# Down projections of the second layer's experts as three float32r products, with the weights' low parts made on GpSimd

## The chip, the cores and the metric

The kernel runs on one core of a Trainium2 chip. The metric is the device time of one launch in microseconds (us). Five engines work side by side, each through its own instructions in order: TensorE (PE, with its weight loads as PEld), VectorE (DVE), ScalarE (ACT), GpSimd (POOL) and SyncE (SP, which here only issues loads). Semaphores order them against each other.

## The reference

Two layers work on 512 latent tokens of width 1024. Each layer has a token mixer (pooling, then attention) and a mixture of 16 SwiGLU experts, of which every token uses two. The change lies in the last line of the mixture, in the second layer only:

```python
def hier_moe(h, w_rg, b_rg, w_re, b_re, w_gate, w_up, w_down):
    ...
    a = jnp.einsum('nd,edf->nef', hf, w_gate)
    b = jnp.einsum('nd,edf->nef', hf, w_up)
    hid = jax.nn.silu(a) * b * gates.astype(h.dtype)[..., None]
    return jnp.einsum('nef,efd->nd', hid, w_down).reshape(shp)
```

An expert is 1024 to 2 x 256 (gate and up) and 256 to 1024 (down), in float32.

## The kernel before

The mixture of a layer (class `Moe`, method `experts`) takes the 16 experts one after the other. In the second layer each expert gets a block of `n` = 96 rows, fetched by index from a copy of the tokens in DRAM (`fetch`, an indirect DMA that GpSimd issues).

**Gate and up.** They are not multiplied in float32. Rows and weights are each split into a high part, rounded to float32r, and a low part, the float32 value less its high part (`split`: ScalarE casts, VectorE or GpSimd subtracts). Three float32r products (high by high, high by low, low by high; `mm3`, L475 to L477) stand for one float32 product. For one expert that is 8 x 3 = 24 products of 512 columns. The weights come as two 1 MB loads, and `ups_steps` splits them in four units of 128 x 1024 into a ring of six buffers, one expert ahead. The rows are turned (8 transposes, L466) and split by `turn`.

**Down.** `turn_hidden` turns the 96 x 256 hidden block into `hT` (two transposes, L767, and one copy by ScalarE, L769). `down` multiplies it with the expert's 1 MB of down weights in float32 (L783: two halves of 512 columns, two products each; the profile shows every float32 product as two MATMUL rows), VectorE multiplies the result with the layer's gate row (L784), and GpSimd issues an indirect DMA that adds the 96 rows to the output in DRAM (L785, called the scatter here; the fetch is L735). Every scatter of this layer adds to the same output, so each waits until the one before has landed.

**The order of a pass.** Pass `e` of the loop in `experts` writes, for each engine, in this order: the first two splits of expert `e + 1`; the 24 products of `up(e)`; the last two splits; the activation and the multiplication of hidden `e`; the fetch for expert `e + 3`; turning and splitting the rows of `e + 1`; `down(e - 1)`; and `turn_hidden(e)`. Every second pass VectorE also builds the one-hot tables that place the next two experts' rows (L713). Each engine keeps this order, so an instruction that waits holds back what is behind it on its engine. SyncE's weight loads are issued when `done` frees a slot of 1 MB.

Of the kernel before, what the change touches and what calls it, by code (L numbers as in the profile page):

```python
# [11 lines left out]
F32R = mybir.dt.float32r  # L12
# [8 lines left out]
D = 1024  # L21
# [7 lines left out]
NE = 16  # L29
# [196 lines left out]
def backbone(ctx: ExitStack, tc: tile.TileContext, a: dict, out: bass.AP):  # L226
    nc = tc.nc
    V, A, G, T = nc.vector, nc.scalar, nc.gpsimd, nc.tensor
# [76 lines left out]
    def done(*key):  # L305
        ar.used.remove((slots.pop(key), SLOT))
        fill()

    def get(*key):
        assert key in slots, key  # L310
        return live[key]
# [68 lines left out]
    for c in range(0, 512 + D, 512):  # L380
        hi = partA[0:64, :]
# [87 lines left out]
    def split(hi, lo, src, eng=V):  # L469

        A.copy(hi, src)  # L471
        eng.tensor_sub(lo, src, hi.bitcast(F32))  # L472
# [12 lines left out]
    class Moe:  # L485
# [277 lines left out]
        def turn_hidden(self, hid):  # L763
            n = self.n
            p = pb.get("t", [128, 2, n])
            for k in range(2):
                T.transpose(p[:, k, :], hid[:, k * 128:k * 128 + 128], ident[:n, :n])  # L767
            hT = self.sb.tile([128, 2, n], name="hidT", bufs=2)
            A.copy(hT, p)  # L769
            return hT  # L770

        def down(self, e, hT, wd):
            n = self.n
            y = self.sb.tile([128, D], name="y", bufs=2)[:n]
            gs = self.g2[0][:n]
            if self.l == 0:
                gs = y
                V.scalar_tensor_tensor(gs, self.g2[1], self.slots[e][2], self.g2[0], op0=OP.mult, op1=OP.add)
            for half in range(2):
                cols = slice(512 * half, 512 * half + 512)  # L780
                p = pb.get("y", [n, 512])
                for k in range(2):
                    T.matmul(p, hT[:, k, :], wd[:, k, cols], start=k == 0, stop=k == 1)  # L783
                V.tensor_mul(y[:, cols], p, gs[:, cols])  # L784
            G.indirect_dma_start(out=self.acc[e % len(self.acc)], out_offset=bass.IndirectOffsetOnAxis(ap=self.slots[e][0], axis=0),  # L785
                                 in_=y, in_offset=None, bounds_check=self.nt * 128 - 1, oob_is_err=False,
                                 compute_op=OP.add)

        def experts(self, acc, caps, more, hooks={}):
            l, nt, sb, mb = self.l, self.nt, self.sb, self.mb  # L790
# [22 lines left out]
            hT = {}  # L813
            for e in range(NE):
                cap(caps[min(e, len(caps) - 1)])
                first = ahead if e == 0 else iter(())
                ahead = group(2) if e == 0 else group(e + 3) if e % 2 and e + 3 < NE else iter(())
                if e:
                    next(ahead, None)
                behind = self.ups_steps(e + 1) if e + 1 < NE else iter(())  # L820
                next(behind, None)
                next(behind, None)

                def later():
                    yield from first
                    if e == 0:
                        yield next(ahead)
                    yield from behind

                hid = self.up(e, self.units.pop(e), later())  # L830
                next(ahead, None)
                for k in range(2 if e == 0 else e + 3, min(e + 4, NE)):
                    self.fetch(k)
                if e + 1 < NE:
                    self.turn(e + 1)
                if e < 2:
                    for _ in range(BESIDE[self.l] if e == 0 else 99):
                        next(more, None)
                if e:
                    self.down(e - 1, hT[e - 1], get("wd", l, e - 1))  # L840
                    done("wd", l, e - 1)
                hT[e] = self.turn_hidden(hid)
                if e == 2:
                    self.count()
                if e in hooks:
                    hooks[e]()
            self.down(e, hT[e], get("wd", l, e))
            done("wd", l, e)
            if NE in hooks:
                hooks[NE]()  # L850

# [6 lines left out]
            units = self.ring[-4:]  # L858
            nb = nc.values_load(self.nb[0:1, 0:1], min_val=0, max_val=2 * nt * 128 // self.n)  # L859
            with tc.For_i(0, nb) as _:  # L860
# [14 lines left out]
                wd = load(a["moe_wd"][l, bass.ds(ev, 1)].rearrange("o p n -> (o p) n"), 2)  # L875
# [16 lines left out]
                    pass  # L892
                self.fetch(NE)
                self.turn(NE)
                self.down(NE, self.turn_hidden(self.up(NE, units)), wd)
                V.tensor_scalar(blk, blk, 1.0, None, op0=OP.add)


# [30 lines left out]
    parts = 0  # L929
# [235 lines left out]
    hT = [hbuf[2], hbuf[3]] + hbuf  # L1165
# [128 lines left out]
    for i in range(17):  # L1294
        kv, t = divmod(i, 4)
        if i < 16:
            p = P[i] = pb.get("q", [128, 256])
# [63 lines left out]
    def wo_mm(p, half, t, k):  # L1361
# [6 lines left out]
    units = [(kv, pair, qh, hh, q2) for kv in range(4) for pair in range(2) for qh in range(2)  # L1368
             for hh in range(2) for q2 in range(2)]
    PT, Ps, mx, po = {}, {}, {}, {}  # L1370
    for step in range(len(units) + 8):
# [3 lines left out]
        if step < len(units):  # L1375
# [4 lines left out]
            p = pb.get("s", [128, 768])  # L1380
            for c0, c1 in ((0, 512), (512, 768)):
                for j in range(2):
                    T.matmul(p[:, c0:c1], qT[kv][:, 2 * pair + hh, q0:q0 + 128], kT[:, kv, j, c0:c1],  # L1383
                             start=j == 0, stop=j == 1)
# [10 lines left out]
        if 3 <= step <= len(units) + 2:  # L1395
# [4 lines left out]
            for g3 in range(2):  # L1400
                p2 = pb.get("t", [128, 3, 128])
                for j in range(3):
                    k = 3 * g3 + j
# [5 lines left out]
        if 7 <= step < len(units) + 7:  # L1409
# [4 lines left out]
            for k in (((), (0, 1), (2, 3), (4, 5)) if qh == 0 else ((0, 1), (2,), (3, 4), (5,)))[quarter]:  # L1414
                for hh in range(2):
                    T.matmul(po[g // 2][64 * hh:64 * hh + 64, 256 * qh:256 * qh + 256],  # L1416
                             vv[:, k, kv * 64:kv * 64 + 64], PT[g, hh][:, k, :],
                             start=k == 0, stop=k == NT - 1, skip_group_check=True)
# [28 lines left out]
    with ar.scope() as sb:  # L1447
# [25 lines left out]
        for t in range(4):  # L1473
            p = pb.get("q", [128, 512])
# [75 lines left out]
```

## Time and profile before

| | |
|---|---|
| median of 3 runs | 923.98 us (922.69 to 924.25) |
| profiled execution, its own time | 923.87 us |
| its span, first to last instruction | 922.1 us |
| busy in the span: PE, PEld, DVE, ACT, POOL | 87%, 59%, 67%, 52%, 18% |
| mean granted TensorE clock | 0.937 |
| second layer's expert loop | about 740 to 908 us of the span |

Busy shares are means over stages that have different limits. What decides a stage is which wait ends last in it, so the rows below are of the second layer's expert loop, and of two earlier places where GpSimd subtracts or adds beside VectorE.

### The profile page before, as it was taken

How to read it: one execution, taken by the hardware profiler on the slowest of the kernel's cores; microseconds unless marked ns; L12 is line 12 of the kernel's file. 1: busy time of each engine (PE TensorE's matmuls, PEld its weight loads, DVE VectorE, ACT ScalarE, POOL GpSimd, SP SyncE). 2: the span in 40 equal slices, each digit the busy share in tenths (PEclk: the TensorE clock that was granted, in tenths of full speed). 3: DMA queues.
4: the chain of work that ended last, by engine and by line, in shares of the span. 5: the costliest groups of instructions: out<-in, count | busy, mean ns of one | idle time of the engine just before them, and what ended most of it. 6: DMA issues, size and time to landing. Idle time of an engine off the chain costs nothing. (4 is left out here: it accounts for less than half of the span.)

```text
span 922.1 us, 12824 instructions
## 1 busy us (share of the span) xinstructions
PE 800.4 (87%) x4593; PEld 540.8 (59%) x4593; DVE 621.1 (67%) x1083; ACT 482.1 (52%) x1006; POOL 169.8 (18%) x164
## 2 busy tenths in 40 slices
PE   4699958989999963998878999999999599999993
PEld 0256735567776512998766656556677355666661
DVE  3453777799999445766656667668436688888761
ACT  2534336345555334665568777768623364555540
POOL 1050332123322310002300000001200222422211
PEclk9879977999999976999998999999999789999997
DMA  8989569999998975602020433220146599999962
GB/s 338 417 309 378 230 222 371 374 307 363 375 351 307 353 250 231 256 16 92 1 93 1 183 131 144 92 92 1 47 159 259 206 375 334 314 339 342 343 219 30
DMA packets 38354, 213.19 MB, mean 231 GB/s; under 512 B 6916, under 2 KB 6996, under 8 KB 18352
## 3 DMA queue, kind: packets, MB, share of 16 engines
q1 hardware_dynamic: 25840, 175.20, 49.5%
q0 software_dynamic: 10032, 27.30, 11.6%
q10 hardware_dynamic: 2416, 9.84, 2.7%
q8 instruction: 37, 0.61, 0.3%
q14 instruction: 29, 0.24, 0.1%
HBM read 193.44 MB, written 30.41 MB: 243 GB/s over the span
## 5 line engine op out<-in xcount | busy, mean ns | idle before, releaser
L475 PE MATMUL banks<-low 128*128 128x512 f32 (+2 forms) x404 | 153.9, 381 | 5.7 <-DVE main L1194 4.2
L476 PE MATMUL banks<-low 128*128 128x512 f32 (+2 forms) x404 | 149.0, 369 | 1.1 <-DVE low L472 1.1
L477 PE MATMUL banks<-low 128*128 128x512 f32 (+2 forms) x404 | 149.2, 369 | 0.0
L472 DVE TENSOR_TENSOR low<-main,low 128x1024 fp32r<-128x1024 f32 (+1 forms) x121 | 129.4, 1128 | 18.3 <-ACT low L471 18.1
L471 ACT CAST low<-main 128x1024 fp32r<-128x1024 f32 (+1 forms) x137 | 119.2, 933 | 2.4 <-issue 1.3
L1387 DVE TENSOR_REDUCE main<-banks 128x1 f32<-128x768 f32 x64 | 61.2, 956 | 43.8 <-PE banks L1383 43.6
L475 PEld LDWEIGHTS banks<-low 128*128 128x128 f32 (+1 forms) x404 | 74.0, 183 | 23.8 <-ACT low L471 6.5
L477 PEld LDWEIGHTS banks<-low 128*128 128x128 f32 (+1 forms) x404 | 73.7, 182 | 17.1 <-DVE low L472 0.8
L476 PEld LDWEIGHTS banks<-low 128*128 128x128 f32 (+1 forms) x404 | 74.1, 183 | 16.0 <-DVE low L472 1.7
L783 PE MATMUL banks<-main 128*128 128x512 f32 (+1 forms) x176 | 80.6, 601 | 0.5 <-ACT main L769 0.5
L472 POOL TENSOR_TENSOR low<-main,low 128x512 fp32r<-128x512 f32 x16 | 20.7, 1296 | 288.1 <-ACT low L471 288.1
L411 PE MATMUL banks<-main,cT 128*32 128x512 f32 x376 | 62.5, 770 | 12.8 <-DMA main<-in_w_mod_dram 10.5
L1405 ACT COPY main<-banks 128x384 f32<-128x384 f32 x128 | 55.9, 486 | 33.7 <-PE banks L1404 33.3
L1408 ACT ACTIVATE main<-banks,main 128x768 f32<-128x768 f32 x64 | 63.8, 996 | 8.4 <-DVE main L1391 3.5
L466 PE MATMUL banks<-ident,main 128*128 128x128 f32 (+2 forms) x384 | 49.6, 273 | 18.0 <-DVE main L1219 13.0
L769 ACT COPY main<-banks 128x256 f32<-128x256 f32 (+1 forms) x32 | 11.1, 346 | 98.4 <-PE banks L767 90.9
L784 DVE TENSOR_TENSOR main<-banks,main 128x512 f32<-128x512 f32 (+1 forms) x64 | 43.1, 687 | 28.8 <-PE banks L783 27.1
L1404 PE MATMUL banks<-ident,main 128*128 128x128 f32 x384 | 54.7, 276 | 3.9 <-ACT mid L1292 2.0
L466 PEld LDWEIGHTS banks<-ident,main 128*128 128x128 f32 (+2 forms) x384 | 42.3, 146 | 24.2 <-DVE main L1219 13.3
L735 POOL DMA_INDIRECT main<-hD,main x32 | 38.1, 1192 | 98.6 <-issue 40.9
L1416 PE MATMUL banks<-main 128*64 128x256 f32 x384 | 53.8, 394 | 2.0 <-DVE low L1394 2.0
L783 PEld LDWEIGHTS banks<-main 128*128 128x128 f32 (+1 forms) x176 | 30.4, 182 | 35.0 <-issue 32.6
(260 smaller groups left out, 1481.0 us busy)
## 6 DMA issues: line engine op xcount, KB each, us to landing
main<-in_moe_wgu_dram SPq DMA_DIRECT2D x50, 1024.0 KB
main<-in_w_mod_dram SPq DMA_DIRECT2D x47, 1024.0 KB
main<-in_moe_wd_dram SPq DMA_DIRECT2D x22, 1024.0 KB
mid<-in_moe_wgu_dram SPq DMA_DIRECT2D x14, 1024.0 KB
mid<-in_moe_wd_dram SPq DMA_DIRECT2D x10, 1024.0 KB
main<-in_attn_wqkv_dram SPq DMA_DIRECT2D x6, 1024.0 KB
hD<-main POOLq DMA_DIRECT2D x9, 512.0 KB, 3.4
main<-in_attn_wo_dram SPq DMA_DIRECT2D x4, 1024.0 KB
```

Source lines behind the costliest of these rows:

```text
L411: T.matmul(p[32 * j:32 * j + 32, :], cT[:, 4 * h + j, :], w[:, j, :], start=h == 0, stop=h == 1)
L466: T.transpose(p[:, k, :], src[:, c * 128:c * 128 + 128], ident[:n, :n])
L471: A.copy(hi, src)
L472: eng.tensor_sub(lo, src, hi.bitcast(F32))
L475: T.matmul(p, xh, wh, start=first, stop=False)
L476: T.matmul(p, xh, wl, start=False, stop=False)
L477: T.matmul(p, xl, wh, start=False, stop=last)
L783: T.matmul(p, hT[:, k, :], wd[:, k, cols], start=k == 0, stop=k == 1)
L1387: V.reduce_max(m[:, 0:1], p, axis=AX.X)
L1404: T.transpose(p2[:, j, :], Ps[u][:, k * 128:k * 128 + 128], ident)
L1405: A.copy(PT[u // 4, hh][:, 3 * g3:3 * g3 + 3, 128 * q2:128 * q2 + 128], p2)
L1408: A.activation(Ps[step], p, AF.Exp, bias=mx[step][:, 0:1], scale=rq, accum_out=mx[step][:, 1:2])
```

## The change

In the second layer (`self.l` is 1) the down projection is done as gate and up are: the hidden block and the down weights are split, and three float32r products stand for each float32 product, so 12 products for one expert. The hidden block's low part is subtracted on VectorE. The weights' high part is cast by ScalarE in two halves, and the low part is subtracted by GpSimd (`down_parts`), except for the last expert, whose two halves VectorE subtracts, into ring buffers that are free by then. The split of the weights of expert `e - 1` is written at the start of pass `e`, after the first split of expert `e + 1`; the slot of the down weights is freed by it. The first layer is as before.

```diff
@@ turn_hidden
+            if self.l:
+                parts = [self.sb.tile([128, 2, n], F32R, name=name) for name in ("hidh", "hidl")]
+                split(*parts, p)
+                return parts
...
+        def down_parts(self, wd, parts=None, eng=G):
+
+            hi, lo = parts or [self.sb.tile([128, 2, D], F32R, name=name) for name in ("wdh", "wdl")]
+            for half in range(2):
+                cols = slice(512 * half, 512 * half + 512)
+                split(hi[:, :, cols], lo[:, :, cols], wd[:, :, cols], eng)
+            return hi, lo
@@ down
-                for k in range(2):
-                    T.matmul(p, hT[:, k, :], wd[:, k, cols], start=k == 0, stop=k == 1)
+                if self.l:
+                    for k in range(2):
+                        for i in range(2):
+                            T.matmul(p, hT[i][:, k, :], wd[0][:, k, cols], start=k == i == 0, stop=False)
+                    for k in range(2):
+                        T.matmul(p, hT[0][:, k, :], wd[1][:, k, cols], start=False, stop=k == 1)
...
@@ experts
                 next(behind, None)
+                if l and e:
+                    wd = self.down_parts(get("wd", l, e - 1))
+                    done("wd", l, e - 1)
+                if l and e == NE - 1:
+                    spare = [self.ring[i].rearrange("p a b n -> p (a b n)").rearrange("p (k n) -> p k n", k=2)
+                             for i in range(6) if i not in [(4 * e + q) % 6 for q in range(4)]]
+                    last = self.down_parts(get("wd", l, e), spare, V)
+                    done("wd", l, e)
                 next(behind, None)
...
-                if e:
+                if e and l:
+                    self.down(e - 1, hT[e - 1], wd)
+                elif e:
                     self.down(e - 1, hT[e - 1], get("wd", l, e - 1))
                     done("wd", l, e - 1)
```

On GpSimd, at the start of the second layer's expert loop, fetches and scatters alternated before (`main` and `mid` hold loaded weights and rows, `low` holds split parts, `out_dram` is the output):

```order
L735 DMA main<-hD,main 96x1024 x3
L785 DMA out_dram<-main 512x1024
L735 DMA main<-hD,main 96x1024
L785 DMA out_dram<-main 512x1024
L735 DMA main<-hD,main 96x1024
```

In the same place of the changed program:

```order
L735 DMA main<-hD,main 96x1024 x2
L472 TENSOR_TENSOR low<-main,low 128x2x512 x2
L735 DMA main<-hD,main 96x1024
L804 DMA out_dram<-main 512x1024
L472 TENSOR_TENSOR low<-mid,low 128x2x512 x2
L735 DMA main<-hD,main 96x1024
L804 DMA out_dram<-main 512x1024
```

Two subtractions of 128 x 1024 now stand behind each scatter and ahead of the next fetch. On ScalarE, one pass in the middle of the loop (`banks` is PSUM) read before:

```order
L758 ACTIVATE main<-banks 96x256
L471 CAST low<-banks 128x384 x2
L769 COPY main<-banks 128x192
L471 CAST low<-main 128x1024 x4
L758 ACTIVATE main<-banks 96x256
```

And it reads now:

```order
L758 ACTIVATE main<-banks 96x256
L471 CAST low<-banks 128x384 x2
L471 CAST low<-banks 128x192
L471 CAST low<-main 128x1024
L471 CAST low<-main 128x2x512 x2
L471 CAST low<-main 128x1024 x3
L758 ACTIVATE main<-banks 96x256
```

The two casts of down weights stand between the first and the second of the four casts for the next expert, and the copy of the hidden block has become a cast.

## Rows read from the trace of the kernel before

**Rows 1.** Windows between scatters' starts (821.16 to 870.97 us), last and sum

```profile
860.98:870.97 9.99, 9.99 (x47) 6.13 (x45) 7.63 (x12) 5.33 (x9) 2.41 (x2) 1.00 0.99 335
sum 49.81, PE 49.81 PEld 30.46 DVE 39.54 ACT 26.55 POOL 12.05; mean PE 9.96 PEld 6.09 DVE 7.91 ACT 5.31 POOL 2.41
```

**Rows 2.** Timeline of PE, 810 to 820 us: start, us, instruction

```profile
810.96 3.60 PE L783 MATMUL banks<-main 128*96 128x512 f32 x8
...
814.40 0.33 PE L767 MATMUL banks<-ident,main 96*128 96x96 f32 x2
...
815.26 0.39 PE L475 MATMUL banks<-low 128*96 128x512 f32 x1
...
819.90 0.40 PE L477 MATMUL banks<-low 128*96 128x512 f32 x1
```

**Rows 3.** Timeline of DVE, 821 to 831 us

```profile
821.56 1.02 DVE L472 TENSOR_TENSOR low<-banks,low 128x384 fp32r<-128x384 f32 x2
823.10 0.69 DVE L784 TENSOR_TENSOR main<-banks,main 96x512 f32<-96x512 f32 x1 [0.52 <-PE banks L783]
824.81 0.69 DVE L784 TENSOR_TENSOR main<-banks,main 96x512 f32<-96x512 f32 x1 [1.03 <-PE banks L783]
826.28 4.63 DVE L472 TENSOR_TENSOR low<-mid,low 128x1024 fp32r<-128x1024 f32 x4 [0.78 <-ACT low L471]
830.96 0.48 DVE L760 SCALAR_TENSOR_TENSOR main<-main,banks 96x256 f32<-96x256 f32 x1
```

**Rows 4.** Timeline of ACT, 825 to 829 us

```profile
824.98 0.32 ACT L769 COPY main<-banks 128x192 f32<-128x192 f32 x1 [3.07 <-PE banks L767]
825.20 3.90 ACT L471 CAST low<-mid 128x1024 fp32r<-128x1024 f32 x4
```

**Rows 5.** Line 515 on POOL: count, ns min/median/max

```profile
L515 POOL TENSOR_TENSOR main<-low x3: 2342/2343/2352, 90.1 to 106.0; 128x1024 f32<-128x1024 f32 x3
```

**Rows 6.** Timeline of POOL, 100 to 109 us

```profile
100.55 3.18 POOL L515 TENSOR_TENSOR mid<-low 128x1024 f32<-128x1024 f32 x1 [5.81 <-DVE low L978]
...
105.98 2.35 POOL L515 TENSOR_TENSOR main<-low 128x1024 f32<-128x1024 f32 x1 [1.72 <-DVE r L1030]
```

**Rows 7.** Timeline of DVE, 100 to 110 us

```profile
100.24 1.28 DVE L520 SCALAR_TENSOR_TENSOR main<-main,r,low 128x1024 f32<-128x1024 f32 x1
102.13 0.69 DVE L977 TENSOR_TENSOR main<-banks,mid 128x512 f32<-128x512 f32 x1 [0.61 <-PE banks L975]
...
106.15 3.27 DVE L520 SCALAR_TENSOR_TENSOR main<-main,r,low 128x1024 f32<-128x1024 f32 x1 [0.18 <-PE banks L466]
```

**Rows 8.** Timelines of POOL and DVE, 423 to 426 us

```profile
423.63 1.29 POOL L472 TENSOR_TENSOR low<-main,low 128x512 fp32r<-128x512 f32 x1 [5.70 <-ACT low L471]
...
423.87 1.33 DVE L1195 TENSOR_TENSOR main<-main 128x256 f32<-128x256 f32 x1
425.67 0.43 DVE L1200 TENSOR_TENSOR main<-main 128x256 f32<-128x256 f32 x1 [0.47 <-ACT main L1199]
```

**Rows 9.** Timeline of POOL, two of the 16 scatters

```profile
798.58 3.46 POOL L785 DMA_INDIRECT out_dram<-main  x1 [8.03 <-DVE low L472]
...
850.95 1.43 POOL L785 DMA_INDIRECT out_dram<-main  x1 [7.26 <-DVE low L472]
```

**Rows 10.** Tile out_dram: its DMAs from issue to landing

```profile
DMA to landing us min/median/max: 5.2/9.1/11.6
```

**Rows 11.** Timelines of DVE and POOL, 894 to 912 us

```profile
894.36 0.69 DVE L784 TENSOR_TENSOR main<-banks,main 96x512 f32<-96x512 f32 x1 [1.03 <-PE banks L783]
...
904.49 1.41 POOL L785 DMA_INDIRECT out_dram<-main  x1 [6.00 <-DVE main L784]
...
910.71 1.41 POOL L785 DMA_INDIRECT out_dram<-main  x1 [4.81 <-DMA out_dram<-main]
```

**Rows 12.** Windows, 740 to 750 us: PE busy first, then the others, granted clock

```profile
740.00:745.00 5.00, 3.89 (x34) 2.98 (x33) 5.00 (x8) 4.69 (x7) 0.14 (x1) 1.00 1.02 415
745.00:750.00 5.00, 4.33 (x21) 0.85 (x19) 3.05 (x8) 1.39 (x3) 1.84 (x2) 0.51 1.00 421
```

More of the change, by code (lines that the diff above doesn't have):

```diff
@@ L781, in down @@
                 p = pb.get("y", [n, 512])
-                for k in range(2):
-                    T.matmul(p, hT[:, k, :], wd[:, k, cols], start=k == 0, stop=k == 1)
+                if self.l:
[4 more added lines that the diff above has]
+                        T.matmul(p, hT[0][:, k, :], wd[1][:, k, cols], start=False, stop=k == 1)
+                else:
+                    for k in range(2):
+                        T.matmul(p, hT[:, k, :], wd[:, k, cols], start=k == 0, stop=k == 1)
                 V.tensor_mul(y[:, cols], p, gs[:, cols])
@@ L846, in experts @@
                     hooks[e]()
-            self.down(e, hT[e], get("wd", l, e))
-            done("wd", l, e)
+            if l:
+                self.down(e, hT[e], last)
+            else:
+                self.down(e, hT[e], get("wd", l, e))
+                done("wd", l, e)
             if NE in hooks:
@@ L894, in experts @@
                 self.turn(NE)
-                self.down(NE, self.turn_hidden(self.up(NE, units)), wd)
+                hidden = self.turn_hidden(self.up(NE, units))
+                self.down(NE, hidden, self.down_parts(wd) if l else wd)
                 V.tensor_scalar(blk, blk, 1.0, None, op0=OP.add)
```

## The prediction

> **What bounds the kernel now.** I read the page's slices first, to find the stage that the change touches: the second layer's expert loop, where PE is busy almost throughout. The windows between scatters' starts give the length of a pass: five passes take 49.81 us, so 9.96 each, and PE is busy in all of it at the full clock of 1.00 (2.4 GHz). DVE is busy 7.91 of 9.96, ACT 5.31, POOL 2.41, and the DMA share is 0.99 [rows 1]. So PE is the bound, but DVE has only 2.05 us to spare in a pass, and the DMA engines have next to nothing. The timeline of PE gives the price of the part that is replaced: the eight float32 rows of one down projection start at 810.96, and the next work starts at 814.40, so they take 3.44 us [rows 2]. The timeline of DVE shows its order within a pass: two subtractions from PSUM (rows), two multiplications from PSUM, then four subtractions of 128 x 1024 with both inputs in SBUF, then the hidden block [rows 3]. The order matters below, because the added work on POOL wants to run while those four run.
>
> **PE.** From 815.26 to 819.90 it makes 20 float32r products of the new shape, 0.232 us each [rows 2]. Twelve take 2.78 us where the float32 form took 3.44: 0.66 us less for an expert, 10.5 us for 16. This is all that the change takes away. PE's need for a pass falls from 9.96 to 9.30.
>
> **ACT.** Two casts of 128 x 1024 for an expert, 3.90 / 4 = 0.98 each [rows 4], and the copy becomes a cast of the same size. 5.31 + 1.96 = 7.3 us, below every pass length here, so it costs nothing by itself.
>
> **DVE.** One more subtraction, 128 x 192 from PSUM. The trace has it only at 128 x 384, 0.51 us [rows 3]; ACT's copy of the very size takes 0.32 [rows 4]. Between nothing (if it fits a wait) and 0.51, I take 0.35. DVE's need: 8.26.
>
> **POOL.** Two subtractions of 128 x 1024 for each of 15 experts. The nearest row is an undisturbed product of that size with both inputs in SBUF, 2.34 us [rows 5]: 4.69 for an expert. With a fetch and a scatter (2.41 together) POOL has 7.1 us to do in a pass, so it isn't the bound on its own account.
>
> **The two together.** This is the term that decides. At 105.98 POOL starts a two-input product of 2.35 us, until 108.33; DVE's two-input instruction that starts at 106.15 takes 3.27 us, until 109.42, where the same one took 1.28 a few us before [rows 6, 7]. It stood still until POOL had ended and then needed the rest. The other way round, POOL's product at 100.55 needs 3.18 us, since DVE's two-input one (100.24 to 101.52) was under way; and while POOL has its turn, DVE's instruction at 102.13, which has one input in PSUM, takes its plain 0.69. In the attention stage the same is seen with `split` itself: POOL's low part runs from 423.63 to 424.92, and DVE's 128 x 256 product takes 1.33 beside it, where its twin takes 0.43 [rows 8]. So a POOL subtraction and a DVE instruction with two SBUF inputs exclude each other, and one with an operand in PSUM doesn't take part. The losses (1.99 of 2.35, 0.90 of 1.29) are less than POOL's whole time only because DVE's instruction came 0.17 and 0.24 us after POOL's; a DVE that is behind loses all of it.
>
> The Trainium skill's page "SBUF — State Buffer", section "Who interferes with whom", states this as a rule: a VectorE instruction with two SBUF inputs and a GpSimd instruction that reads SBUF share an interface, whoever issues first has it for the whole instruction, and the other is blocked, not slowed. By the rule all of POOL's time comes onto a DVE that always has such an instruction queued. By the row with the least loss (1.33 - 0.43 = 0.90 of POOL's 1.29, or 70%) it would be 3.27 of 4.69 a pass, and the sum below would give 946 instead of 966.
>
> What of the 4.69 can lie beside DVE's PSUM work? That work is 1.02 + 0.69 + 0.69 + 0.48 = 2.88 us a pass [rows 3]. But POOL gets its inputs from ACT's casts, and those come behind the hidden block's cast and one cast for the next expert: with 824.98 as the start, 0.32 + 0.98 + 0.98 later, at 827.3, at the earliest [rows 4]. By then DVE's second multiplication (to 825.50) is over and its four subtractions have begun (826.28) [rows 3]. The next PSUM work stands behind all four of them on DVE. And the hidden block is behind them too; PE's next two transposes wait for it, ACT's next round of casts waits for those, so the delay doesn't shrink from pass to pass. I therefore take no cover: a pass needs 7.91 + 0.35 + 4.69 = 12.95 us of DVE's time, with DVE as the bound, and PE waiting for 3.65 of it. With full cover it would be 12.95 - 2.88 = 10.07. The upper end is POOL's own waiting: a scatter that met DVE's subtractions took 3.46 instead of 1.43 [rows 9], which pushes the two subtractions behind it by up to 2 us; half of that may reach the pass, 1 us.
>
> **Loads.** The down weights are now needed at the start of a pass, ahead of the 24 products (5.6 us), not behind them, and SP's next load goes into their slot, so it waits for POOL's second subtraction and holds SP's two other loads behind it. With passes of 10 us and a DMA share of 0.99 this would be a new wait; with 13 us the same bytes take 76% of the pass, which covers it. If the pass stayed at 10, I could not cost this at nothing.
>
> **The end.** Now the second multiplication of expert 13 ends at 895.05, scatter 14 starts at 904.49, scatter 15 at 910.71 [rows 11]. After the change there stand between the same two events scatter 13 itself (1.43), two POOL subtractions (4.69), DVE's two for expert 15, which may come between them (nothing to 2.3), two products (0.46) and the multiplication (0.69): 7.3 to 9.6 us, against 9.44 now. Scatter 15 waits for 14 to land, as before. I take no change.
>
> **The sum.** Passes 1 to 14 have both POOL's and DVE's subtractions: 14 x (12.95 - 9.96) = 41.9 us. The profiled execution took 923.87, 0.1 below the median of the runs: 923.87 + 41.9 = 965.8, so 966 us. With the upper end of 1 us a pass it is 980.
>
> **Rivals.**
> *Half hidden.* DVE issues its four subtractions back to back, and POOL might get its turn only in gaps: the scatter of 3.46 us in [rows 9] sat beside several of them. Then one of POOL's two falls behind the fourth, beside PSUM work, and costs nothing: 10.61 us a pass, 933. DVE would still wait for ACT's two added casts between its first and second subtraction, up to 1.96, which half cancels that: 11.6, 947. Say 940. Against it: in [rows 6, 7] POOL had its turn as soon as the one DVE instruction was over.
>
> *PE's clock falls.* PE would wait 3.6 us in a pass. From 740 to 745 it was busy for 3.89 of 5 us with tiny products and waits among them, and from 745 the granted clock is 0.51 (1.2 GHz) [rows 12]. At that level the 24 products of gate and up take 5.57 us more; PE has 3.65 to spare, so 1.9 a pass: 966 + 27 = 993. Against it: the dense 24 products in each pass, which held the clock at 1.00 through [rows 1]. The Trainium skill's "TensorE: Matmul & The Clock Gate", Part 1, says that the slow level is the default and activity lifts it, which would allow this; no row here shows a pass of 72% PE at either level.
>
> *Scatters bind, no change.* If POOL's subtractions disturbed nobody, each scatter would still wait for the one before to land, 9.1 us at the median [rows 10], and the starts are 9.96 apart, so a pass would stay where it is. POOL's subtractions stand behind it, so PE couldn't run ahead: 922 to 926.
>
> *Faster.* PE remains the bound, POOL's work hides, and scatters land sooner: 16 x 0.66 = 10.5, so 913. It holds if a pass of DVE and POOL stays under 9.30, that is if no more than 1.0 of the 4.69 stands in DVE's way (8.26 + 1.0). [Rows 8] speak against it.
>
> **Chances.** No cover 0.64, half hidden 0.18, clock 0.08, scatters bind 0.05, faster 0.05. The range, 936 to 986, holds the first with its upper end and most of the second. About 0.2% (1.8 us) is what a measurement of this kernel tells from no change: slower 0.90, within it 0.05, faster 0.05.
>
> **What the profile after would show.** Windows between scatters of about 13 us, DVE busy or standing in all but a little of it, PE at some 72%. DVE's 128 x 1024 subtractions and POOL's new ones together 4.7 us longer for a pass than 4 x 1.16, in long rows of one or the other, with ends that coincide. The down products at 0.23 us each. I am wrong if DVE's subtractions keep their 1.16 us and POOL's 2.34, or if passes are under 11 us, or if the loop's granted clock isn't 1.00.

## The result

The changed kernel takes 975.42 us (median of 4 runs, 971.89 to 978.00) where the kernel before, on the same chip, takes 924.12: a ratio of 1.054, 95% interval 1.051 to 1.058. The forecast was 966, with a range of 936 to 986. The profiled execution took 971.89 us with a span of 970.1; before it was 923.87 and 922.1.

To compare kernels I use one stretch throughout: ten passes, from VectorE's hidden-block instruction (L760) of expert 4 to that of expert 14. Its first and last starts are in a row of the trace, and one window between them shows all engines. First the window of the kernel before, for this stretch (longer than that of [rows 1]; columns: length, then busy time of PE, PEld, DVE, ACT and POOL with instructions, granted clock, DMA share, GB/s):

```profile
790.90:890.70 99.80, 99.80 (x455) 61.10 (x454) 79.25 (x111) 53.28 (x81) 22.80 (x18) 1.00 0.95 323
```

The changed kernel: its L760 (count, ns min/median/max, first and last start) and its ten passes:

```profile
L760 DVE SCALAR_TENSOR_TENSOR main<-main,banks x11: 462/466/467, 803.6 to 939.3; 96x256 f32<-96x256 f32 x11
```

```profile
803.60:939.30 135.70, 106.58 (x492) 72.77 (x492) 123.33 (x121) 71.78 (x100) 83.90 (x38) 0.91 0.71 237
```

So a pass went from 9.98 to 13.57 us. The place of the 48.0 us between the spans follows: 35.9 in these ten passes, 12.7 before them (803.6 against 790.9), and -0.6 behind them (970.1 - 939.3 = 30.8 against 922.1 - 890.7 = 31.4). DVE is busy 12.33 in a pass and waits 1.24; PE waits 2.9, and its granted clock is 0.91 in the mean and no longer 1.00. The DMA share fell from 0.95 to 0.71, so the loads have room.

Where DVE's time went is seen in the groups of line 472, the subtractions (ns min/median/max; the first row is PSUM work, the two others have both inputs in SBUF):

```profile
L472 DVE TENSOR_TENSOR low<-banks,low x40: 335/540/544, 762.8 to 941.8; 128x384 fp32r<-128x384 f32 x26, 128x192 fp32r<-128x192 f32 x14
L472 DVE TENSOR_TENSOR low<-main,low x38: 1205/1213/6537, 763.6 to 938.2; 128x1024 fp32r<-128x1024 f32 x38
...
L472 DVE TENSOR_TENSOR low<-mid,low x14: 1208/1214/6571, 786.3 to 924.8; 128x1024 fp32r<-128x1024 f32 x14
```

The medians are about what they were ([rows 3]: 4.63 for four), the maxima are 6.5 us. One subtraction of a pass stands still behind POOL's pair, and the others aren't touched. Two neighbouring passes show how, first the longer one (timelines of POOL and DVE: start, length):

```profile
861.48 3.36 POOL L804 DMA_INDIRECT out_dram<-main  x1 [4.21 <-DVE low L472]
864.40 5.21 POOL L472 TENSOR_TENSOR low<-main,low 128x1024 fp32r<-128x1024 f32 x2
...
861.39 1.01 DVE L713 TENSOR_TENSOR main<-slot,main 128x384 bf16<-128x384 f32 x2
862.32 1.21 DVE L472 TENSOR_TENSOR low<-mid,low 128x1024 fp32r<-128x1024 f32 x1
864.15 6.57 DVE L472 TENSOR_TENSOR low<-mid,low 128x1024 fp32r<-128x1024 f32 x1 [0.62 <-ACT low L471]
...
876.11 1.43 POOL L804 DMA_INDIRECT out_dram<-main  x1 [1.22 <-DVE low L472]
877.13 5.19 POOL L472 TENSOR_TENSOR low<-main,low 128x1024 fp32r<-128x1024 f32 x2
...
876.14 1.23 DVE L472 TENSOR_TENSOR low<-main,low 128x1024 fp32r<-128x1024 f32 x1
878.98 4.43 DVE L472 TENSOR_TENSOR low<-main,low 128x1024 fp32r<-128x1024 f32 x1 [1.62 <-ACT low L471]
```

POOL's two subtractions run as one block of 5.2 us, of which the first 0.4 still overlap the scatter's row (861.48 + 3.36 = 864.84). DVE's instruction ends 1.1 us after the block, at 870.72 and at 883.41, which is about its own time: it got next to nothing done before. In the first pass it was ready at 864.15 and lost 5.4 us; in the second DVE waited for ACT until 878.98 while POOL's block was already under way, and lost 3.2. The first pass takes 14.63 us, the second 12.37. Passes of these two kinds alternate through most of the loop; three of the ten passes, with scatters of 2.4 us, take about 13.4:

```profile
861.48:876.11 14.63, 11.33 (x55) 7.93 (x54) 13.96 (x15) 7.05 (x11) 9.12 (x5) 0.85 0.77 264
876.11:888.48 12.37, 10.65 (x51) 7.33 (x51) 10.72 (x11) 7.39 (x11) 8.01 (x4) 0.96 0.82 281
```

In the long kind the scatter's descriptors take 3.36 in place of 1.43 us, so POOL's block starts 2.92 us behind the scatter's start and not 1.02. Both kinds have a DVE subtraction beside the scatter; in all of the ten passes its time goes with which of them came first. Three scatters start 0.03 us ahead of DVE's subtraction (876.11, 876.14), and both take their plain time. Seven start 0.06 to 0.09 us behind DVE's two-input work (861.48, with the one-hot tables of L713 from 861.39 and a subtraction to 863.53), and end 1.3 us behind that subtraction.

PE's longest waits have the same source (waits between 763 and 942: total, times, longest; the second row is DVE's own wait):

```profile
PE banks L767 <- DVE low L472: 32.5, 12, 3.8
...
DVE low L472 <- ACT low L471: 16.0, 14, 1.6
```

PE can't transpose the hidden block (L767) until DVE has made it, and DVE makes it behind its four subtractions.

### The profile page after: what moved, and what is told of

It is laid out like the page before. It is cut to its first block, busy times and chain, and to the rows that moved or that the text cites. A ratio compares the mean times of both kernels' runs of the same rounds, so it can differ in the third digit from the quotient of the medians.

```text
span 970.1 us, 13049 instructions
## 1 busy us (share of the span) xinstructions
PE 807.5 (83%) x4657; PEld 558.8 (58%) x4657; DVE 686.9 (71%) x1101; ACT 511.5 (53%) x1038; POOL 256.3 (26%) x194
## 5 line engine op out<-in xcount | busy, mean ns | idle before, releaser
L472 DVE TENSOR_TENSOR low<-main,low 128x1024 fp32r<-128x1024 f32 (+1 forms) x121 | 174.1, 1488 | 31.1 <-ACT low L471 30.7
L475 PE MATMUL banks<-low 128*128 128x512 f32 (+2 forms) x404 | 159.6, 395 | 6.0 <-DVE main L1227 4.5
L472 POOL TENSOR_TENSOR low<-main,low 128x1024 fp32r<-128x1024 f32 (+1 forms) x38 | 79.2, 2203 | 289.8 <-ACT low L471 289.8
L476 PE MATMUL banks<-low 128*128 128x512 f32 (+2 forms) x404 | 154.4, 382 | 1.1 <-DVE low L472 1.1
L477 PE MATMUL banks<-low 128*128 128x512 f32 (+2 forms) x404 | 154.1, 381 | 0.0
L471 ACT CAST low<-main 128x1024 fp32r<-128x1024 f32 (+1 forms) x159 | 140.8, 949 | 3.9 <-issue 2.3
L471 ACT CAST low<-banks 128x512 fp32r<-128x512 f32 (+2 forms) x84 | 38.4, 496 | 108.6 <-PE banks L767 40.2
L475 PEld LDWEIGHTS banks<-low 128*128 128x128 f32 (+1 forms) x404 | 76.9, 190 | 25.9 <-ACT low L471 6.8
L477 PEld LDWEIGHTS banks<-low 128*128 128x128 f32 (+1 forms) x404 | 76.5, 189 | 18.7 <-issue 1.1
L476 PEld LDWEIGHTS banks<-low 128*128 128x128 f32 (+1 forms) x404 | 77.0, 191 | 17.5 <-DVE low L472 1.7
L735 POOL DMA_INDIRECT main<-hD,main x32 | 41.6, 1299 | 110.5 <-issue 29.4
L466 PEld LDWEIGHTS banks<-ident,main 128*128 128x128 f32 (+2 forms) x384 | 42.2, 146 | 25.8 <-DVE main L1252 13.4
L472 DVE TENSOR_TENSOR low<-mid,low 128x1024 fp32r<-128x1024 f32 x30 | 49.5, 1681 | 3.6 <-ACT low L471 3.5
L472 DVE TENSOR_TENSOR low<-banks,low 128x512 fp32r<-128x512 f32 (+2 forms) x84 | 44.8, 565 | 6.8 <-ACT low L471 6.5
L804 POOL DMA_INDIRECT out_dram<-main x16 | 33.7, 2107 | 52.2 <-DVE low L472 47.6
```

The source lines that it names most:

```text
L466: T.transpose(p[:, k, :], src[:, c * 128:c * 128 + 128], ident[:n, :n])
L475: T.matmul(p, xh, wh, start=first, stop=False)
L476: T.matmul(p, xh, wl, start=False, stop=False)
L477: T.matmul(p, xl, wh, start=False, stop=last)
```

## The experiments

Each kernel was timed in turns with the kernel before on the same chip, at medians of 924.91, 924.70 and 924.46 us in the three sets. "A pass" is a tenth of the ten passes.

**Does the preparation alone cost it?** The float32 products and the plain hidden block of before; the preparation stays, and nobody reads it.

```diff
-                if self.l:
-                    for k in range(2):
-                        for i in range(2):
-                            T.matmul(p, hT[i][:, k, :], wd[0][:, k, cols], start=k == i == 0, stop=False)
...
+                for k in range(2):
+                    T.matmul(p, hT[:, k, :], wd[:, k, cols], start=k == 0, stop=k == 1)
...
-                    wd = self.down_parts(get("wd", l, e - 1))
-                    done("wd", l, e - 1)
+                    self.down_parts(get("wd", l, e - 1))
```

> The kernel before, with its float32 down products and its plain hidden block, to which only the preparation of the changed kernel is added: ScalarE's two casts of the down weights and Pool's two subtractions for each expert, which nobody uses. Theory (exclusion): nearly the whole loss comes from these, 962 to 985 us, and VectorE's 128 x 1024 subtractions take 2.1 us at the mean. Rival (the three products, the split of the hidden block, or TensorE that waits for the two parts): 924 to 935.

Measured: 976.31 us, ratio 1.055 (1.052 to 1.058), the same as the changed kernel. Its ten passes:

```profile
809.40:942.90 133.50, 109.93 (x452) 65.51 (x452) 118.83 (x111) 71.55 (x100) 82.79 (x38) 0.92 0.71 240
```

ACT's casts and POOL's subtractions cost all of it. The products and the split of the hidden block cost nothing on top, and their saving is not seen either.

**Is it POOL's time, or its reading?** POOL fills the low part for as long as the subtraction would take, and reads nothing.

```diff
-                split(hi[:, :, cols], lo[:, :, cols], wd[:, :, cols], eng)
+                A.copy(hi[:, :, cols], wd[:, :, cols])
+                low = lo[:, :, cols].bitcast(F32)
+                G.memset(low, 0.0)
+                G.memset(low, 0.0)
+                G.memset(low[:, half:, :], 0.0)
```

> The changed kernel, in which Pool fills the low part of the down weights with zeros, two and a half times for each half (about 2.4 us, the time of the subtraction), and reads nothing from SBUF; VectorE still subtracts for the last expert no more. The low part of the down weights is left out of the result by that. Theory (exclusion): an instruction that reads no SBUF input excludes nobody, VectorE keeps 1.16 to 1.22 us for its subtractions, and the time is 918 to 930. Rival (Pool's time itself: 7.1 us of work in a pass in front of the scatters and fetches, whatever it does): 960 to 980.

The fills also don't wait for ACT's casts, and the last expert's two subtractions on VectorE (about 2.3 us) are gone too.

Measured: 935.71 us, ratio 1.011 (1.008 to 1.013). This is 6 us above what the theory gave, and 40 us below the changed kernel. The timelines of POOL and DVE in one pass, and the ten passes:

```profile
843.83 1.45 POOL L783 MEMSET low<- 128x1024 f32 x1
845.34 0.95 POOL L784 MEMSET low<- 128x1024 f32 x1
846.35 0.95 POOL L785 MEMSET low<- 128x1024 f32 x1
...
843.95 3.50 DVE L472 TENSOR_TENSOR low<-mid,low 128x1024 fp32r<-128x1024 f32 x3 [1.29 <-ACT low L471]
```

```profile
796.00:900.20 104.20, 99.19 (x492) 65.86 (x491) 80.50 (x122) 70.69 (x100) 79.27 (x80) 1.00 0.91 309
```

POOL is about as busy as in the changed kernel (79 us in the ten passes, 84 there), and DVE's three subtractions take 3.50 us, undisturbed. So it is not POOL's time or the queue on POOL, it is that POOL reads SBUF. The Trainium skill's page "SBUF — State Buffer", section "Who interferes with whom", has this distinction: a VectorE instruction with two SBUF inputs collides with a GpSimd instruction that reads SBUF and not with one that only writes; the trace agrees (3.50 us for three here, 6.57 for one there). The pass is still 0.44 longer than before. In the ten passes PE waits 5.0 us, 3.5 of them for POOL's fills, which stand before the products that read the low part; whether the rest of the change would cost as much this kernel doesn't settle.

**The low part on VectorE.**

```diff
-                    wd = self.down_parts(get("wd", l, e - 1))
+                    wd = self.down_parts(get("wd", l, e - 1), eng=V)
```

> The changed kernel, with the low parts of the down weights subtracted on VectorE and not on Pool; the order of the code is the same. Theory (a Pool subtraction and a VectorE instruction with two SBUF inputs exclude each other, so 4.69 us of Pool's time came onto VectorE in each pass): VectorE now has 7.91 + 0.35 + 2 x 1.16 = 10.58 us to do in a pass, so 14 x 0.62 = 8.7 us over the kernel before, 933 us; up to 942 if VectorE also waits for ScalarE's casts. Its 128 x 1024 subtractions all take 1.16 to 1.22 us. Rival (ScalarE's added casts, the earlier need of the down weights, or gaps on TensorE with a falling clock are what costs): those are all still there, so it stays at 965 to 978.

Measured: 937.03 us, ratio 1.015 (1.010 to 1.021), inside what the theory gave.

```profile
796.40:901.90 105.50, 96.95 (x494) 67.68 (x493) 101.36 (x142) 71.16 (x100) 55.31 (x20) 0.98 0.89 305
```

DVE is busy 10.14 of 10.55 us in a pass: it is the bound, as worked out (10.58). Giving POOL the work made the engine that it was to relieve lose 4.1 us a pass (12.33 - 7.93 - 0.35), where doing it there costs 2.3.

**Half of it on POOL.**

```diff
-                split(hi[:, :, cols], lo[:, :, cols], wd[:, :, cols], eng)
+                A.copy(hi[:, :, cols], wd[:, :, cols])
+                if half == 0:
+                    eng.tensor_sub(lo[:, :, cols], wd[:, :, cols], hi[:, :, cols].bitcast(F32))
...
-                    for k in range(2):
+                    for k in range(2 if half == 0 else 0):
```

> The changed kernel, in which Pool subtracts the low part for the first 512 columns alone; the low part of the other half, and its two products, are left out of the result. Theory (exclusion, Pool's 2.34 us onto VectorE for each subtraction): 7.91 + 0.35 + 2.34 = 10.6 us of VectorE in a pass, the same as with both halves subtracted on VectorE, so the time of that kernel within 5 us: 932 to 942. Rival (what costs is the chain from cast to Pool to the products, or the order on Pool, and one subtraction pays most of it): 950 or more.

Measured: 942.27 us, ratio 1.019 (1.013 to 1.024), a pass 11.40; 0.3 us above the theory's upper end. The first subtraction with its products costs 17 us over no low part at all (925.23, below), the second another 33. DVE is busy 10.05 us of a pass here and waits 1.28 for ACT, together 11.33. That the first subtraction eats the room that DVE had beside PE, and the second finds none, is how I read it; no run shows it apart.

**One input or two on POOL.** POOL copies the rounded half.

```diff
-                split(hi[:, :, cols], lo[:, :, cols], wd[:, :, cols], eng)
+                A.copy(hi[:, :, cols], wd[:, :, cols])
+                eng.tensor_copy(lo[:, :, cols], hi[:, :, cols].bitcast(F32))
```

> The changed kernel, in which Pool copies the rounded half into the place of the low part, with one SBUF input in place of the subtraction's two; the low part of the down weights is left out of the result (a copy of the high part stands for it). Theory (a Pool instruction that reads SBUF excludes VectorE's two-input one, with one input as well as with two): VectorE's subtractions again take 2 us and more beside it, and the time lies above the kernel whose Pool only writes (936) by what the copies last, 945 to 980. Rival (only Pool's second input excludes VectorE): VectorE's subtractions keep 1.22 us, 925 to 940.

Measured: 938.75 us, ratio 1.015 (1.009 to 1.020). The time lies in the rival's range, but the rival's mechanism is not there:

```profile
857.08 1.53 POOL L782 CAST low<-low 128x1024 fp32r<-128x1024 f32 x1
857.08 2.51 POOL L782 CAST low<-low 128x1024 fp32r<-128x1024 f32 x2
...
857.80 2.88 DVE L472 TENSOR_TENSOR low<-main,low 128x1024 fp32r<-128x1024 f32 x1 [1.56 <-ACT low L471]
```

DVE's subtraction ends at 860.68, 1.09 after POOL's pair (859.59), so here a reader with one input blocked it as well. The time is short because the pair takes 2.51 us and not 5.2; I had not priced the copy.

**The scatter behind the subtractions.**

```diff
-            G.indirect_dma_start(out=self.acc[e % len(self.acc)], ...
+            def scatter():
+                G.indirect_dma_start(out=self.acc[e % len(self.acc)], ...
+            if self.l and e < NE - 2:
+                self.put = scatter
+            else:
+                scatter()
...
                     done("wd", l, e - 1)
+                    if e > 1:
+                        self.put()
```

> The changed kernel, with each scatter issued behind the two Pool subtractions of the next pass and not ahead of them (the last two stay where they are). Theory: a scatter's descriptors that meet VectorE's two-input work take 3.36 in place of 1.43 us and hold Pool's subtractions back, which is the difference of about 2.2 us between alternate passes of the changed kernel; with the subtractions first, the long passes fall to the short ones: 958 to 967. Rival (the pass is long by Pool's subtractions alone, and the alternation is VectorE's own extra work in every second pass): 970 to 980.

Measured: 962.32 us, ratio 1.041 (1.035 to 1.046), inside what the theory gave. The alternation is all but gone (windows between scatters 12.67 and 12.08):

```profile
803.60:926.20 122.60, 103.12 (x492) 70.95 (x492) 110.37 (x122) 71.34 (x100) 93.52 (x40) 0.93 0.76 262
```

A pass is 12.26, so the scatter's place ahead of the subtractions costs 1.3 us in each. That isn't the stretched descriptors alone: in this kernel POOL's pair no longer runs as one block either (last section), and the edit changes both at once.

**The long third pass.** The pass from 775.46 takes 18.61 us, the longest. One expert's low part goes to VectorE, the one that stands there.

```diff
-                    wd = self.down_parts(get("wd", l, e - 1))
+                    wd = self.down_parts(get("wd", l, e - 1), eng=V if e == 3 else G)
```

> The changed kernel, with the low parts of one expert (the third) subtracted on VectorE and all others on Pool. Theory: the pass of 18.61 us between the second and the third scatter is long because a 128 x 16 operation with two SBUF inputs stood for 5.26 us beside Pool's pair; it falls to 12 to 14 us, and the time to 968 to 972. Rival (that pass is long by the counting of tokens itself, as it was longer before, too: 12.71): 974 to 978.

Measured: 972.80 us, ratio 1.054 (1.051 to 1.056), between the theory's range and the rival's and in neither; its interval overlaps that of the changed kernel, so the times don't separate them. The traces say more. In the changed kernel (timelines of DVE and POOL):

```profile
776.05 0.18 DVE L646 TENSOR_TENSOR main<-main 128x16 f32<-128x16 f32 x1
776.26 0.17 DVE L645 TENSOR_SCALAR main<-banks 128x16 f32<-128x16 f32 x1
776.47 5.26 DVE L646 TENSOR_TENSOR main<-main 128x16 f32<-128x16 f32 x1
...
776.46 5.23 POOL L472 TENSOR_TENSOR low<-main,low 128x1024 fp32r<-128x1024 f32 x2
```

In this kernel, all of that line, and the window of the pass:

```profile
L646 DVE TENSOR_TENSOR main<-main x4: 174/176/176, 780.3 to 781.5; 128x16 f32<-128x16 f32 x4
```

```profile
780.11:795.91 15.80, 11.87 (x53) 8.00 (x52) 14.92 (x44) 7.04 (x11) 2.43 (x3) 0.82 0.73 239
```

The standing of 5.26 us is gone; the pass still takes 15.80, above the theory's 12 to 14, since DVE now has two more subtractions beside the counting. So both the theory and the rival have a part.

**The clock.** Twelve more products in each pass, to keep PE at work while it waits.

```diff
+                if l and e >= 2:
+                    p = pb.get("m", [self.n, 512])
+                    xh = self.slots[e][4][0]
+                    for _ in range(12):
+                        T.matmul(p, xh[:, 0, :], xh.rearrange("p a b -> p (a b)")[:, :512], start=True, stop=True)
                 hid = self.up(e, self.units.pop(e), later())
```

> The changed kernel with 12 more float32r products of 512 columns at the head of each of passes 2 to 15, whose results nobody uses; they stand in the 1.5 to 3.8 us in which TensorE waits, about 2.8 us at the full clock. Theory (VectorE and Pool set the pass, and the lower granted clock, 0.85 to 0.96 in the mean of a pass, hides in TensorE's waits): the granted clock rises or not, the time stays within 970 to 982. Rival (the slower products are on the path of each pass): 945 to 965.

Measured: 975.87 us, ratio 1.054 (1.049 to 1.060): no change. Two of its windows between scatters:

```profile
865.12:879.77 14.65, 13.18 (x71) 9.26 (x70) 13.33 (x16) 8.12 (x12) 9.14 (x5) 1.00 0.71 219
879.77:893.15 13.38, 12.16 (x60) 8.46 (x59) 11.81 (x11) 7.42 (x11) 9.01 (x5) 1.00 0.86 287
```

These are one pass with a scatter of 3.36 us and one with 2.42. The changed kernel's passes with such scatters are as long at a lower clock: 14.63 at 0.85 (above), and this one at 0.88:

```profile
848.07:861.48 13.41, 10.94 (x48) 7.43 (x47) 11.79 (x11) 7.30 (x11) 9.04 (x5) 0.88 0.71 254
```

With PE's waits filled the granted clock is 0.98 over the ten passes, for 0.91, and the time is the same. So the lower clock goes with PE's waits and costs nothing there.

**What was there to gain?** No low part of the weights at all: no subtraction for it, 8 products in place of 12.

```diff
-                split(hi[:, :, cols], lo[:, :, cols], wd[:, :, cols], eng)
+                A.copy(hi[:, :, cols], wd[:, :, cols])
...
-                    for k in range(2):
-                        T.matmul(p, hT[0][:, k, :], wd[1][:, k, cols], start=False, stop=k == 1)
```

> The changed kernel without the low part of the down weights: no subtraction for it on any engine, and 8 float32r products for an expert in place of 12. That part is left out of the result. Theory (exclusion): only ScalarE's casts, the hidden block's low part on VectorE and the earlier need of the weights are left beside a shorter TensorE (8 x 0.232 = 1.86 us for 3.44), so 908 to 924: the scatters' landing (9.1 us at the median before) or the loads may keep a pass near 9.96. Rival (casts, loads or the hidden block's split are what costs): 940 or more.

Measured: 925.23 us, ratio 1.000 (0.998 to 1.002). The 25 us that PE saves (16 x 1.58) don't show at all. The ten passes in halves:

```profile
795.10:841.40 46.30, 44.37 (x242) 31.31 (x241) 40.55 (x64) 36.14 (x52) 12.01 (x8) 1.00 0.99 337
841.40:897.60 56.20, 45.13 (x222) 30.96 (x220) 38.56 (x60) 35.60 (x50) 13.49 (x10) 0.97 0.90 305
```

Five passes of 9.26 us, and then five of 11.24. In the second half ACT's casts wait for the down weights (waits, 850 to 900):

```profile
ACT low L782 <- DMA main<-in_moe_wd_dram: 4.5, 2, 2.4
ACT low L782 <- DMA mid<-in_moe_wd_dram: 4.3, 2, 2.2
```

Whether the loads are the reason was asked with two kernels that load half of each down weight:

```diff
-            load = nc.sync.dma_start(ar.at(off, [128, SLOT]), src)
+            part = SLOT // 2 if key[:2] == ("wd", 1) else SLOT
+            load = nc.sync.dma_start(ar.at(off, [128, SLOT])[:, :part], src[:, :part])
```

On top of the kernel without low part:

> The kernel without the low part of the down weights (8 products, no subtraction for it), which also loads only the first half of each down weight of the second layer; the other half is whatever lay in the buffer, so those rows of the weights are left out of the result. Theory (there the loads set the 10 us pass, 3 MB of weights and the rows): with a sixth of the weights' bytes gone the pass falls towards TensorE's 8.4 and VectorE's 8.3 us, 900 to 916. Rival (scatters, or waits between the engines, set it): 920 to 927.

On top of the kernel before:

> The kernel before, which loads only the first half of each down weight of the second layer; the other half is whatever lay in the buffer, so those rows of the weights are left out of the result. Theory (TensorE, busy in all of the 9.96 us, is a bound of its own there beside the loads): 918 to 925, passes of 9.6 to 10 us. Rival (TensorE was only held up by the loads): passes near 9.3 us or less and 915 or below.

Measured: 916.52 us for the first, ratio 0.993 (0.991 to 0.995), 0.5 us above the theory's upper end; 925.06 for the second, 1.001 (0.999 to 1.003), on the theory's upper end. Their ten passes, in this order:

```profile
788.90:880.80 91.90, 87.53 (x462) 61.38 (x460) 79.18 (x122) 71.40 (x102) 27.87 (x18) 1.00 0.88 289
```

```profile
792.30:892.10 99.80, 99.80 (x456) 61.13 (x454) 79.23 (x111) 53.31 (x82) 34.72 (x18) 1.00 0.86 272
```

With fewer bytes the passes stay at 9.19 throughout, so in the kernel without low part the loads made the later passes long. Why those are even longer than the 9.98 of before, with the same bytes, stays open. The kernel before keeps its 9.98 with half the down weights: there PE is the bound, as the prediction had it. And 9.19 is not the 8.4 of PE's work (9.98 - 1.58). PE is busy 8.75 of it, 0.35 more than that, for a reason that no run shows, and it now waits about 0.5 us a pass for the hidden block (waits of the first of the two kernels), for which it has no such row before.

```profile
PE banks L768 <- DVE low L473: 4.9, 10, 0.5
```

**A mixture.** Half the columns in the new form, with VectorE making their low part.

```diff
-            for half in range(2):
-                cols = slice(512 * half, 512 * half + 512)
-                split(hi[:, :, cols], lo[:, :, cols], wd[:, :, cols], eng)
-            return hi, lo
+            split(hi, lo, wd[:, :, 0:512], eng)
+            return hi, lo, wd
...
-                if self.l:
+                if self.l and half == 0:
...
+                    u, v = (hT[2], wd[2]) if self.l else (hT, wd)
...
-                    wd = self.down_parts(get("wd", l, e - 1))
-                    done("wd", l, e - 1)
+                    wd = self.down_parts(get("wd", l, e - 1), eng=V)
```

> Only the first 512 columns of a down projection are three float32r products, with the low part on VectorE; the other 512 stay two float32 products; Pool does nothing more than in the kernel before. VectorE has 7.91 + 0.35 + 1.16 = 9.42 us in a pass, TensorE 9.96 - 0.33 = 9.63. If TensorE alone bound the kernel before: 14 x 0.33 = 4.6 us less, 918 to 921. Rival (the loads, with a DMA share of 0.99, bound it as much, so a shorter TensorE gives nothing back): 922 to 930.

Measured: 930.16 us, ratio 1.007 (1.003 to 1.010): 0.2 us above the rival's upper end, and slower than before by 0.7%. A pass is 10.26. PE's weight loads wait for DVE there (waits, 800 to 890):

```profile
PEld banks L767 <- DVE low L472: 9.0, 9, 1.0
```

No arrangement of this change that loads all its weights beat the kernel before.

## Why the prediction was right, and where its sizes were off

**The mechanism held.** The added preparation is all of the loss (976.31 with the old products), POOL's reading beside DVE's two-input subtractions is about 40 of its 51 us (975.42 - 935.71, where POOL only writes), and DVE is busy or standing for 12.33 us of a pass of 13.57. The forecast took "no cover" over "half hidden", and the passes of 12.4 to 14.6 us bear that out.

**The size of a pass: 12.95 forecast, 13.57 measured.** Three terms moved. In DVE's time the pass is 7.93 of the old work, 0.35 for the hidden block, 4.05 standing and 1.24 waiting; the third term below is inside these, not beside them.
- *DVE standing for POOL.* 4.69 was taken, 4.1 measured. The price of POOL's work was right: from the scatter's end the pair takes 4.8 us (864.84 to 869.61), for 4.69 from [rows 5]. But DVE can lose more than that, 5.4 in the long passes, where it stands while the scatter's descriptors end. The cover was too low: I reasoned that POOL's inputs come too late for anything but DVE's subtractions, but in six of the ten passes POOL's block began while DVE waited for ACT.
- *That wait.* "It costs nothing by itself" was said of ACT's two added casts. ACT is indeed busy only 7.18 of 13.57 us, but its casts for the weights stand ahead of those for the next expert, and DVE waits for ACT 16.0 us in 14 waits, 1.14 each. It was named under the rival "half hidden" and left out of the forecast's own sum; this is the step that was wrong.
- *The scatter's descriptors.* They were put at an upper end of 1 us a pass and at nothing in the forecast. The scatter's place ahead of the pair costs 1.3 (13.57 - 12.26): four of the ten scatters take 3.36 us and three 2.4, and with them goes part of the cover. With the scatter behind the pair DVE is busy 11.04 us of a pass, 1.3 less, and waits 1.22, as before; so the term is all in DVE's standing. Without it a pass is 12.26, less than forecast, and the time is 962, since the first passes cost more than forecast (next point).

The standing was put 0.6 us too high and the wait 1.2 too low, so that 975 lies near 966 is partly luck.

**A reading of [rows 6 to 8].** The losses were said to fall short of POOL's whole time only because DVE came 0.17 and 0.24 us later. They fall short by 0.36 (2.35 - 1.99) and 0.39 (1.29 - 0.90). The rest, 0.19 and 0.15, is that DVE's instruction ended 1.09 and 0.28 us behind POOL's, less than the 1.28 and 0.43 of its plain time. The step that was built on it, that a DVE which comes later loses all of POOL's time, changes little by that.

**The first passes.** The forecast took 14 passes alike. Of the 48 us, 35.9 stand in the ten passes and 12.7 in those before; the third alone gave 5.9 (775.46 to 794.07 is 18.61, and 773.65 to 786.36 before is 12.71), mostly through a 128 x 16 instruction that no term of the sum named: a small two-input instruction on DVE stood as long as a large one.

**PE.** The products come at 0.23 us as forecast, but no kernel here got the saving of 0.66 an expert. The float32 form's 3.44 us covered the way from the end of gate and up to the hidden block; a shorter down projection uncovers some of it (0.5 us a pass with 8 products and half the down weights loaded), and with all the weights loaded the later passes wait for them. So the rival "faster", 913, had little room; with 12 products and nobody in DVE's way it was not tried.

**Clock, loads, tail.** The loop's granted clock was to be 1.00 and is 0.91, a sign of being wrong by the prediction's own list; but the rival that priced it at 27 us was wrong as well, since it costs nothing (the kernel with twelve more products). It shows in PE's busy time alone: 10.66 us a pass, or 79%, where 9.30 and 72% were forecast. The loads were hidden as said, with a DMA share of 0.71 for a forecast of 0.76. The end took 0.6 us less, for a forecast of no change. Scatters land in 6.7 us at the median now, from 9.1 [rows 10], and hold up nothing in the ten passes:

```profile
DMA to landing us min/median/max: 5.2/6.7/8.7
```

**The rule on who is first.** The prediction cited the Trainium skill's page "SBUF — State Buffer", section "Who interferes with whom": whoever issues first has the interface. At 864.15 DVE's subtraction issued 0.25 us ahead of POOL's first, and it still waited for both; by the rule it should have gone before them, and the measurement decides. POOL's descriptors were under way until 864.84 and may have held the interface for the work behind them; that is argued, not shown. For it speaks that every block counted in the last section came straight behind descriptors, against it that the scatter at 876.11 held up no subtraction of DVE (1.23 us at 876.14).

## What to carry to other kernels

Before giving work to an idle GpSimd, look at what VectorE does at that moment: here GpSimd's subtractions held up VectorE's two-input instructions in SBUF for up to their whole duration, so the engine that was to be relieved paid 4.1 us a pass for work it could have done in 2.3. Fills that only wrote SBUF held up none. And a bound engine's busy time is a gain only as far as nothing is close behind it: here 1.58 us less of PE's work for an expert gave nothing with all the weights loaded, and 0.8 with half of the down weights, where PE waited 0.5 for the hidden block.

## What was not expected

**Descriptors are held up as well.** In the kernel with the low part on VectorE, six subtractions stand in a row on DVE, and a fetch of 96 rows that POOL issues beside them takes 8.48 us in place of 0.98 (timelines of POOL and DVE):

```profile
840.98 8.48 POOL L735 DMA_INDIRECT main<-hD,main  x1 [0.30 <-issue]
...
841.72 1.21 DVE L472 TENSOR_TENSOR low<-mid,low 128x1024 fp32r<-128x1024 f32 x1
842.86 2.35 DVE L472 TENSOR_TENSOR low<-main,low 128x1024 fp32r<-128x1024 f32 x2
845.13 3.49 DVE L472 TENSOR_TENSOR low<-mid,low 128x1024 fp32r<-128x1024 f32 x3
```

It ends at 849.46, 0.84 us after the last of them (848.62). In the ten passes of that kernel PE waits 4.5 us for rows that such fetches bring.

**POOL's pair is a block in one kernel, and takes turns with DVE in another.** In the changed kernel POOL's pair is one block of 5.2 us in 13 of 15 passes. With the scatter behind the pair they take turns:

```profile
856.77 3.49 POOL L472 TENSOR_TENSOR low<-main,low 128x1024 fp32r<-128x1024 f32 x1 [2.18 <-ACT low L471]
856.77 6.81 POOL L472 TENSOR_TENSOR low<-main,low 128x1024 fp32r<-128x1024 f32 x2 [2.18 <-ACT low L471]
...
858.61 2.72 DVE L472 TENSOR_TENSOR low<-mid,low 128x1024 fp32r<-128x1024 f32 x1 [0.63 <-ACT low L471]
```

DVE's instruction ends at 861.33, 1.07 after POOL's first (860.26) and ahead of its second, which then lasts until 863.58. What decides between the two was not tried, but the traces split by what is ahead of the pair. In the changed kernel and in that of the first experiment 26 pairs of 30 are blocks, and all 26 come straight behind a scatter's descriptors. The four that take turns are the first pair of each kernel, with no scatter ahead (751.08 in the changed kernel, 6.48 us), and two where a DVE subtraction was still running when the descriptors ended (764.56 in the changed kernel, 5.88 us). In the kernel with the scatter behind the pair none comes straight behind descriptors, and no DVE subtraction stands through both.
